# A two-layer attention and convolution trunk on one core: the order inside an attention step, and the parts of the norms' sums

## The chip, the cores and the metric

The kernel runs on one core of one Trainium2 chip. A core has a matrix engine (TensorE, PE in the profile), a vector engine (VectorE, DVE), a scalar engine (ScalarE, ACT), GpSimd (POOL), a queue engine that issues transfers here (SyncE, SP), and 16 DMA engines. The metric is the device time of one execution in microseconds; less is better. Three executions of the kernel before took 1157.65, 1158.02 and 1159.11 us: the median is 1158.02 us.

## The reference

A trunk of two layers works on 256 latent tokens (x, 1024 channels) with 256 context tokens (xc). All values are float32.

```python
for l in range(DEPTH):                                  # DEPTH = 2
    sh1, sc1, g1, sh2, sc2, g2 = split(silu(c) @ w_ada[l] + b_ada[l])      # and the same for the context
    h = rmsnorm(x, norm1_g[l]) * (1 + sc1) + sh1
    p = h @ w_in[l]                                     # conv part, q, k, v, branch gates
    q, k = rope_2d(q), rope_2d(k)                       # 8 heads of 64
    y_conv = silu(layernorm(dwconv31(a * sigmoid(g)))) @ w_conv_out[l]
    y_attn = softmax(q k' / 8 + bias over a window of the latent keys, and all context keys) v @ w_na_out[l]
    x = x + g1 * ((sigmoid(p_gate) * [y_conv, y_attn], summed) @ w_out[l])
    h2 = rmsnorm(x, norm2_g[l]) * (1 + sc2) + sh2
    u = dwconv3(h2 @ w_up[l]);  x = x + g2 * ((silu(u_g) * u_a) @ w_down[l])
    # the context tokens take the same path in layer 0; in layer 1 only their k and v are needed
return rmsnorm(x, final_norm_g)
```

The norms are the sums of squares over all channels of a token: `rsqrt(mean(x*x) + eps)`.

## The kernel before

**Layout.** Channels lie on the 128 partitions (8 tiles for 1024 channels), tokens on the free axis: 512 columns in layer 0 (latents and context are two "streams" of 256 columns) and mostly 256 in layer 1. Each weight comes in units of 1024 columns. SP loads a unit (`raw`, 4 buffers), ScalarE rounds it (`whi`, L148), VectorE takes the remainder (`wlo`, L149), and TensorE multiplies in three matmuls for each tile (`mm3`, L167 to L169: high times high, high times low, low times high; their output tile is called main). The activations are split likewise.

**Order of the work.** The main products are emitted in order, with `slot()` between groups of them. Each call of `slot()` advances every generator in the list `side` by one piece: the attention's steps, the 31 convolution taps, the vector of modulations (adaLN, L194 and L236), and the norms. A scheduler of the tile framework then gives each engine its instruction order; waits between engines follow from the tiles.

**The norm (SumSq L298, rstd L328, norm L362).** Each channel tile's squares (ScalarE, L316) are added to an accumulator (VectorE, L320). The last of the tiles isn't added: it is a second part, squared on VectorE for 256 columns (L312) and on ScalarE for 512. `rstd` sums over the 128 channels by matmuls with a column of ones: for each 128 tokens one product per part, all accumulating (L334; the trace shows each as two instructions). VectorE scales the sum (L336), GpSimd raises it to the power −1/2 (L338), and TensorE spreads it over partitions by transposes (L343). The callers: the first norm (`ss0`), the LayerNorm of the convolution branch (L754, one in each layer), the norms after the output projection (two streams in layer 0, one in layer 1), the ones after the down-projection of layer 0 (two streams), and the final norm, after that of layer 1. A modulated norm (L349) then makes each channel tile's high and low part by L357 to L359.

**Attention (L375).** A pair of heads j gives two or, in layer 0, three items: latent queries 0 to 127, 128 to 255, and all context queries. Scores (L419): six matmuls of 64 rows and 512 columns into two banks of the tag sc (both banks that it has). Softmax (L427 to L435): VectorE adds a bias and takes the maximum, ScalarE does exp and the scaling. Transposes (L469) of the probabilities, with copies by ScalarE (L470). Values (L488): 8 program matmuls of 64 output rows into the tag po (one bank). `step()` (L401) is called once a slot; while items are queued it works only on every second call, and then it does the values due, the transposes due (three calls after the scores), and one queued item's scores, in this order. `ahead` (L391) forces steps until few enough items of the pairs before are left; it is called by `qk` (L657), which makes one pair's q and k on the main products (rotary on VectorE L671 to L674, splits L677 and L678).

**Layer 1's up-projection (L900 on).** Its first four units start on the raw, not yet normalised activations: eight rounds k of 4 products. The generator `sums` (rstd of the norm) is started after round 0 and completed (`whole`) after round 2.

Of the kernel before, what the change touches and what calls it, by code (L numbers as in the profile page):

```python
# [8 lines left out]
F32 = mybir.dt.float32  # L9
# [35 lines left out]
def trunk(ctx: ExitStack, tc: tile.TileContext, xt, cvec, wall, wada, params, bias_t, rope_t, out):  # L45
# [13 lines left out]
    def nm(s):  # L59
        uid[0] += 1  # L60
        return f"{s}_{uid[0]}"
# [3 lines left out]
    def psum(tag="main"):  # L65
        return psp.tile([P, 512], F32, tag=tag, bufs=BANKS[tag], name=nm(tag))
# [7 lines left out]
    def sl(w, i):  # L74
        return w[:, i * P : (i + 1) * P]
# [222 lines left out]
    class SumSq:  # L298


        def __init__(self, T, at):
            self.T, self.n = T, 0
            self.acc = at
            self.parts = [self.acc]

        def add(self, src, last=False):
            T = self.T
            if self.n == 0:
                act.activation(self.acc[:, :T], src, AF.Square)
            elif last and T == S:  # L310
                q = tmp()[:, :T]
                dve.tensor_tensor(q, src, src, ALU.mult)  # L312
                self.parts.append(q)
            else:
                q = tmp()[:, :T]
                act.activation(q, src, AF.Square)  # L316
                if last:
                    self.parts.append(q)
                else:
                    dve.tensor_tensor(self.acc[:, :T], self.acc[:, :T], q, ALU.add)  # L320
            self.n += 1

    def sum_squares(n, T):

        at = tp.tile([P, 512], F32, tag="ss", name=nm("ss"))
        return [SumSq(T, at[:, i * T : (i + 1) * T]) for i in range(n)]

    def rstd(ss, n, bank):  # L328

        nt = ss.T // P  # L330
        pt = psum("pt")
        for t in range(nt):
            for i, p in enumerate(ss.parts):
                pe.matmul(pt[:, t : t + 1], sl(p, t), one, start=i == 0, stop=i == len(ss.parts) - 1)  # L334
        red = small([P, nt], "red")
        mid = dve.tensor_scalar(red, pt[:, :nt], 1.0 / n, EPS, ALU.mult, ALU.add)  # L336
        rs = small([P, nt], "rs")
        pool.tensor_tensor(rs, red, mhalf[:, :nt], ALU.pow)  # L338
        yield mid
        yield  # L340
        pb = psum(bank)
        for t in range(nt):
            pe.transpose(sl(pb, t), rs[:, t : t + 1].to_broadcast([P, P]), ident)  # L343
        return pb
# [30 lines left out]
    class Attention:  # L375
# [4 lines left out]
        def pair(self, j, q, k, bts):  # L380
            po = []
            lat, cx = [None, None], [None, None]
            for qt in range(2):
                self.todo.append((j, qt, q, k, bts[qt], po, lat))
            if self.T > S:
                self.todo.append((j, None, q, k, None, po, cx))

# [3 lines left out]
        def ahead(self, j, n):  # L391

            while sum(it[0] <= j for it in self.todo) > n:
                self.step()

# [4 lines left out]

        def step(self):  # L401
            self.n += 1
            for e in self.soft + self.pv:
                e[0] += 1
            if self.todo and self.n % 2:
                return
            if self.pv and self.pv[0][0] >= 1:
                self.pv.pop(0)[1]()
            if self.soft and self.soft[0][0] >= 3:
                self.turn(*self.soft.pop(0)[1:])  # L410
            if self.todo:
                it = self.todo.pop(0)
                (self.scores if it[1] is not None else self.ctx_scores)(it)

# [5 lines left out]

        def scores(self, it):
            j, qt, q, k, bt, po, pts = it
            out = [psum("sc") for _ in range(2)]
            self.product(out, q, k, slice(qt * P, (qt + 1) * P), slice(0, 2 * S))
            pps = []
# [12 lines left out]

        def ctx_scores(self, it):
            j, qt, q, k, bt, po, pts = it  # L440
            out = [psum("sc") for _ in range(2)]
            for t in range(2):
                self.product([ps[:, t * S : (t + 1) * S] for ps in out], q, k, slice(S + t * P, S + (t + 1) * P), CTX)
            pps = []
# [52 lines left out]

    (ss0,) = sum_squares(1, 2 * S)
    for k in range(KD):
# [4 lines left out]
    for l in range(DEPTH):  # L504
# [5 lines left out]
        with ExitStack() as e1a:  # L510
# [68 lines left out]
            with ExitStack() as e1b:  # L579
# [77 lines left out]
                def qk(j):  # L657

                    att.ahead(j - 2, 0)
                    att.ahead(j - 1, 1 + (T > S))  # L660
                    bts = [eb.tile([P, 2, S], F32, tag="bias", bufs=3, name=nm("bias")) for _ in range(2)]
                    for qt, bt in enumerate(bts):
# [183 lines left out]
        with ExitStack() as e2:  # L846
# [39 lines left out]
            if last:  # L886

                for k in range(KD):
                    for w, ps in zip(first, pss):
                        mm3(ps[:, : S + 2], w[k], h2[0][k][:, RAW], h2[1][k][:, RAW], k == 0, k == KD - 1)  # L890
                    if k == 0:
                        next(sums)
                    if k == 2:
                        pb = whole(sums)
# [37 lines left out]
            if not last:  # L932
                h1 = h_tiles()
            sss = sum_squares(NS, S)
            NB = 0 if last else KD - 2
# [144 lines left out]
```

## Time and profile before

| what | value |
|---|---|
| median of three executions | 1158.02 us |
| the profiled execution | 1160.25 us |
| its span in the profile | 1158.5 us |
| granted TensorE clock, mean | 0.995 |
| read from memory, mean | 161 GB/s |
| share of the transfer queue (q1) of 16 DMA engines' span | 51.3% |

The profiled execution took 1.75 us more than its span, and 2.23 us more than the median. A main matmul starts 0.232 us (512 columns) or 0.118 us (256) after the one before it, though its row shows a longer duration, since matmuls overlap. So what one costs is read from the difference of two starts. The waits of an engine are in its own table: for each wait, the line that waited, the line that released it, the sum, the number and the longest. In a row of the timeline, the first number is the start, the second the duration, x the number of instructions joined to one row, and the brackets hold the idle time before it and what ended it.

### The profile page before, as it was taken

To read this page: it belongs to the slowest core of one execution; us is meant where nothing else is said; L and a number is where in the kernel's file an instruction comes from. 1 tells how busy PE (TensorE), PEld (TensorE's weight loads), DVE (VectorE), ACT (ScalarE), POOL (GpSimd) and SP (SyncE) were. 2 spreads that over 40 slices of the span, in tenths; PEclk is the share of its full clock that TensorE was granted. 3 is DMA by queue.
4 is the path that set the end of the run, shared out by engine and by line. 5 is a ranking of instruction groups with operands and counts; after the bars stand their busy time and mean duration, and the time that the engine had idled before them with its cause. 6 is when DMAs were issued, how large, how long until landed. Compare 5 with 4: busy or idle time off the path is not lost.

```text
span 1158.5 us, 18238 instructions
## 1 busy us (share of the span) xinstructions
PE 1142.6 (99%) x7006; PEld 978.1 (84%) x7006; DVE 951.8 (82%) x1794; ACT 557.6 (48%) x916; POOL 24.6 (2%) x25
## 2 busy tenths in 40 slices
PE   8999999999999999999999999999999999999997
PEld 7677777788769978888888888998879999999996
DVE  3589999968865899988989588789998799888753
ACT  4356667323243354343344222453677567666541
POOL 0000000100000000000000000000000000000000
PEclk8999999999999999999999999999999999999999
DMA  7852313442681345676755455654435474666561
GB/s 242 302 156 79 96 60 110 127 146 60 229 270 60 99 147 171 205 232 201 237 183 160 130 164 180 202 190 132 142 93 163 142 219 125 212 193 183 186 182 55
DMA packets 54230, 187.17 MB, mean 162 GB/s; under 512 B 6272, under 2 KB 6272, under 8 KB 54144
## 3 DMA queue, kind: packets, MB, share of 16 engines
q1 hardware_dynamic: 54144, 186.02, 51.3%
q8 instruction: 55, 0.90, 0.3%
q14 instruction: 31, 0.25, 0.1%
HBM read 184.95 MB, written 1.05 MB: 161 GB/s over the span
## 4 chain that ended last, share of the span: by engine, by line
PE 75%; issue 17%; DVE 3%; DMA 3%; ACT 2%; POOL 0%; SPq 0%; POOLq 0%; DVEq 0%; ACTq 0%
PE main L167 21%; PE main L169 20%; PE main L168 20%; DMA raw<-in_wall 2%; PE po L488 2%; PE sc L419 1%; PE main L589 1%; PE main L590 1%; PE main L591 1%; DVE wlo L149 1%; PE pt L236 1%; PE sc L169 1%; PE pt L334 1%; PE sc L168 1%; PE sc L167 1%
## 5 line engine op out<-in xcount | busy, mean ns | idle before, releaser
L167 PE MATMUL main<-h,whi 128*128 128x256 f32 (+1 forms) x1328 | 450.9, 340 | 1.1 <-ACT whi L148 1.1
L169 PE MATMUL main<-h,wlo 128*128 128x256 f32 (+1 forms) x1328 | 444.1, 335 | 0.1
L168 PE MATMUL main<-h,whi 128*128 128x256 f32 (+1 forms) x1328 | 442.9, 334 | 0.0
L148 ACT CAST whi<-raw 128x1024 fp32r<-128x1024 f32 (+1 forms) x247 | 255.1, 1035 | 341.7 <-PE main L168 171.5
L149 DVE TENSOR_TENSOR wlo<-raw,whi 128x1024 fp32r<-128x1024 f32 (+1 forms) x247 | 296.3, 1204 | 85.8 <-ACT whi L148 84.1
L167 PEld LDWEIGHTS main<-h,whi 128*128 128x128 f32 x1328 | 249.7, 188 | 36.3 <-issue 7.9
L169 PEld LDWEIGHTS main<-h,wlo 128*128 128x128 f32 x1328 | 249.9, 188 | 28.8 <-DVE wlo L149 0.8
L168 PEld LDWEIGHTS main<-h,whi 128*128 128x128 f32 x1328 | 250.2, 188 | 27.0 <-issue 0.6
L259 DVE SCALAR_TENSOR_TENSOR acc<-raw,sil,acc 128x256 f32<-128x256 f32 (+1 forms) x294 | 143.3, 534 | 1.1
L537 DVE SCALAR_TENSOR_TENSOR cb<-u,par,cb 128x512 f32<-128x512 f32 (+1 forms) x240 | 140.2, 611 | 0.6
L167 PE MATMUL main<-fh,whi 128*128 128x256 f32 (+1 forms) x396 | 127.2, 321 | 0.0
L169 PE MATMUL main<-fh,wlo 128*128 128x256 f32 (+1 forms) x396 | 126.4, 319 | 0.0
L168 PE MATMUL main<-fl,whi 128*128 128x256 f32 (+1 forms) x396 | 126.4, 319 | 0.0
L169 PEld LDWEIGHTS main<-fh,wlo 128*128 128x128 f32 x396 | 74.5, 188 | 5.9
L168 PEld LDWEIGHTS main<-fl,whi 128*128 128x128 f32 x396 | 74.5, 188 | 5.7
L167 PEld LDWEIGHTS main<-fh,whi 128*128 128x128 f32 x396 | 74.5, 188 | 5.7
L859 ACT ACTIVATE t<-main,par 128x512 f32<-128x512 f32 (+1 forms) x82 | 50.7, 667 | 13.4 <-PE main L169 13.4
L860 DVE SCALAR_TENSOR_TENSOR t<-main,par,t 128x510 f32<-128x510 f32 (+1 forms) x82 | 47.5, 614 | 1.9 <-ACT t L859 1.5
L863 DVE SCALAR_TENSOR_TENSOR t<-main,par,t 128x510 f32<-128x510 f32 (+1 forms) x82 | 46.8, 610 | 0.0
L799 DVE SCALAR_TENSOR_TENSOR x<-main,mod,x 128x256 f32<-128x256 f32 x48 | 22.2, 480 | 28.1 <-PE main L169 28.1
L358 ACT ACTIVATE h<-t,mod 128x256 fp32r<-128x256 f32 x56 | 25.3, 501 | 35.7 <-DVE t L357 35.7
L878 ACT CAST fh<-t 128x512 fp32r<-128x512 f32 (+1 forms) x44 | 22.5, 513 | 32.6 <-DVE t L875 31.9
(162 smaller groups left out, 1265.0 us busy)
## 6 DMA issues: line engine op xcount, KB each, us to landing
raw<-in_wall SPq DMA_DIRECT2D x239, 512.0 KB, 4.2
raw<-in_wada SPq DMA_DIRECT2D x96, 512.0 KB, 4.3
bias<-in_bias_t SPq DMA_DIRECT2D x16, 256.0 KB, 3.6
x<-in_xt SPq DMA_DIRECT2D x8, 256.0 KB, 4.7
raw<-in_wall SPq DMA_DIRECT2D x8, 256.0 KB, 6.0
out<-t SPq DMA_DIRECT2D x4, 256.0 KB, 2.5
rope<-in_rope_t SPq DMA_DIRECT2D x2, 256.0 KB, 5.3
par<-in_params SPq DMA_DIRECT2D x1, 352.0 KB, 5.6
```

Source lines behind the costliest of these rows:

```text
L148: act.copy(hi[:, c], r[:, c])
L149: dve.tensor_tensor(lo[:, c], r[:, c], hi[:, c].bitcast(F32), ALU.subtract)
L167: pe.matmul(ps, w[0], xh, start=start, stop=False)
L168: pe.matmul(ps, w[0], xl, start=False, stop=False)
L169: pe.matmul(ps, w[1], xh, start=False, stop=stop)
L259: dve.scalar_tensor_tensor(a, w, c, a, ALU.mult, ALU.add)
L358: act.activation(hi[:, c], y[:, c], AF.Identity, bias=b)
L488: pe.matmul(po[i * HD : (i + 1) * HD, c], self.V[kt][:, h * HD : (h + 1) * HD], pts[i][:, kt - kts[0], :], start=kt == kts[0], stop=kt == ...
L537: dve.scalar_tensor_tensor(cb[j], src, w, cb[j], ALU.mult, ALU.add)
L859: act.activation(c, pv_, AF.Identity, bias=pr(l, FDB + t, 1), scale=w[1])
L860: dve.scalar_tensor_tensor(c[:, :, 1:], pv_[:, :, : S - 1], w[0], c[:, :, 1:], ALU.mult, ALU.add)
L863: dve.scalar_tensor_tensor(c[:, :, : S - 1], pv_[:, :, 1:], w[2], c[:, :, : S - 1], ALU.mult, ALU.add)
```

## The change

It has three parts.

1. A sum of squares has a second part only for the first norm and the final one (`apart`). For the seven others, the last tile's squares are taken on ScalarE and added to the accumulator on VectorE like those of the other tiles, and `rstd` has one part. The loops of `rstd` change places.
2. `Attention.step` issues the scores' products first, then the values, then the transposes; the softmax of the scores comes last. An item's scores come at the earliest two calls of `step` after it was queued, unless `ahead` forces them (`now`). In `qk`, the threshold of the pair before is 2 in both layers (1 in layer 1 until now), and layer 1 has four buffers for the bias in place of three.
3. In layer 1's up-projection, `sums` is started after round 1 and completed after round 3.

```diff
@@ -298,8 +298,8 @@
     class SumSq:
 
 
-        def __init__(self, T, at):
-            self.T, self.n = T, 0
+        def __init__(self, T, at, apart):
+            self.T, self.n, self.apart = T, 0, apart
             self.acc = at
             self.parts = [self.acc]
 
@@ -307,31 +307,34 @@
             T = self.T
             if self.n == 0:
                 act.activation(self.acc[:, :T], src, AF.Square)
-            elif last and T == S:
+            elif last and T == S and self.apart:
                 q = tmp()[:, :T]
                 dve.tensor_tensor(q, src, src, ALU.mult)
                 self.parts.append(q)
             else:
                 q = tmp()[:, :T]
                 act.activation(q, src, AF.Square)
-                if last:
+                if last and self.apart:
                     self.parts.append(q)
                 else:
                     dve.tensor_tensor(self.acc[:, :T], self.acc[:, :T], q, ALU.add)
             self.n += 1
 
-    def sum_squares(n, T):
+    def sum_squares(n, T, apart=False):
 
         at = tp.tile([P, 512], F32, tag="ss", name=nm("ss"))
-        return [SumSq(T, at[:, i * T : (i + 1) * T]) for i in range(n)]
+        return [SumSq(T, at[:, i * T : (i + 1) * T], apart) for i in range(n)]
 
     def rstd(ss, n, bank):
 
         nt = ss.T // P
         pt = psum("pt")
-        for t in range(nt):
-            for i, p in enumerate(ss.parts):
-                pe.matmul(pt[:, t : t + 1], sl(p, t), one, start=i == 0, stop=i == len(ss.parts) - 1)
+        for i, p in enumerate(ss.parts):
+            for t in range(nt):
+                pe.matmul(
+                    pt[:, t : t + 1], sl(p, t), one, start=i == 0 and t == 0, stop=i == len(ss.parts) - 1,
+                    skip_group_check=True,
+                )
         red = small([P, nt], "red")
         mid = dve.tensor_scalar(red, pt[:, :nt], 1.0 / n, EPS, ALU.mult, ALU.add)
         rs = small([P, nt], "rs")
@@ -381,9 +384,9 @@
             po = []
             lat, cx = [None, None], [None, None]
             for qt in range(2):
-                self.todo.append((j, qt, q, k, bts[qt], po, lat))
+                self.todo.append((j, qt, q, k, bts[qt], po, lat, self.n))
             if self.T > S:
-                self.todo.append((j, None, q, k, None, po, cx))
+                self.todo.append((j, None, q, k, None, po, cx, self.n))
 
         def busy(self):
             return self.todo or self.soft or self.pv
@@ -391,26 +394,31 @@
         def ahead(self, j, n):
 
             while sum(it[0] <= j for it in self.todo) > n:
-                self.step()
+                self.step(True)
 
         def run(self):
             while True:
                 self.step()
                 yield
 
-        def step(self):
+        def step(self, now=False):
+
+
             self.n += 1
             for e in self.soft + self.pv:
                 e[0] += 1
-            if self.todo and self.n % 2:
+            if self.todo and self.n % 2 and not now:
                 return
+            it = None
+            if self.todo and (now or self.n - self.todo[0][-1] >= 2):
+                *it, _ = self.todo.pop(0)
+                out = self.products(it)
             if self.pv and self.pv[0][0] >= 1:
                 self.pv.pop(0)[1]()
             if self.soft and self.soft[0][0] >= 3:
                 self.turn(*self.soft.pop(0)[1:])
-            if self.todo:
-                it = self.todo.pop(0)
-                (self.scores if it[1] is not None else self.ctx_scores)(it)
+            if it:
+                (self.scores if it[1] is not None else self.ctx_scores)(it, out)
 
         def product(self, out, q, k, c, d):
 
@@ -418,10 +426,18 @@
                 for o, r in zip(out, HALF):
                     pe.matmul(o, q[r, a, c], k[r, b, d], start=n == 0, stop=n == 2)
 
-        def scores(self, it):
+        def products(self, it):
             j, qt, q, k, bt, po, pts = it
             out = [psum("sc") for _ in range(2)]
-            self.product(out, q, k, slice(qt * P, (qt + 1) * P), slice(0, 2 * S))
+            if qt is not None:
+                self.product(out, q, k, slice(qt * P, (qt + 1) * P), slice(0, 2 * S))
+            else:
+                for t in range(2):
+                    self.product([ps[:, t * S : (t + 1) * S] for ps in out], q, k, slice(S + t * P, S + (t + 1) * P), CTX)
+            return out
+
+        def scores(self, it, out):
+            j, qt, q, k, bt, po, pts = it
             pps = []
             for i, ps in enumerate(out):
                 dve.tensor_tensor(ps[:, :S], ps[:, :S], bt[:, i, :], ALU.add)
@@ -436,11 +452,7 @@
                 pps.append(pp)
             self.soft.append([0, it, pps])
 
-        def ctx_scores(self, it):
-            j, qt, q, k, bt, po, pts = it
-            out = [psum("sc") for _ in range(2)]
-            for t in range(2):
-                self.product([ps[:, t * S : (t + 1) * S] for ps in out], q, k, slice(S + t * P, S + (t + 1) * P), CTX)
+        def ctx_scores(self, it, out):
             pps = []
             for ps in out:
                 mx = small([P, 2], "mx2")
@@ -495,7 +507,7 @@
                 dve.tensor_tensor(self.ol[j][:, c], po[:, c], self.oh[j][:, c].bitcast(F32), ALU.subtract)
 
 
-    (ss0,) = sum_squares(1, 2 * S)
+    (ss0,) = sum_squares(1, 2 * S, True)
     for k in range(KD):
         sp.dma_start(x[k], xt[k])
         ss0.add(x[k], k == KD - 1)
@@ -657,8 +669,8 @@
                 def qk(j):
 
                     att.ahead(j - 2, 0)
-                    att.ahead(j - 1, 1 + (T > S))
-                    bts = [eb.tile([P, 2, S], F32, tag="bias", bufs=3, name=nm("bias")) for _ in range(2)]
+                    att.ahead(j - 1, 2)
+                    bts = [eb.tile([P, 2, S], F32, tag="bias", bufs=4 if last else 3, name=nm("bias")) for _ in range(2)]
                     for qt, bt in enumerate(bts):
                         with tc.issue_after(lastdma[0].ins):
                             sp.dma_start(bt, bias_t[l, j, :, qt])
@@ -888,9 +900,9 @@
                 for k in range(KD):
                     for w, ps in zip(first, pss):
                         mm3(ps[:, : S + 2], w[k], h2[0][k][:, RAW], h2[1][k][:, RAW], k == 0, k == KD - 1)
-                    if k == 0:
+                    if k == 1:
                         next(sums)
-                    if k == 2:
+                    if k == 3:
                         pb = whole(sums)
                 for k in range(KD):
                     modulated(l, pb, 4, 3, k, h2, (0,))
@@ -931,7 +943,7 @@
 
             if not last:
                 h1 = h_tiles()
-            sss = sum_squares(NS, S)
+            sss = sum_squares(NS, S, last)
             NB = 0 if last else KD - 2
             if not last:
                 ad = ada_vector([(1, j, True, 2) for j in range(0, 8)])
```

On the engines' instruction orders, the change has these effects beside the removed L334. In layer 0 the attention's steps stay in their places, with the order inside each changed. In layer 1 the scores and values stand in 10 separate stretches of TensorE's order where there were 13. One adaLN product (L194) in layer 0, after the attention, stands in two halves. In the norm after layer 1's output projection, 24 main matmuls stand between round 1's end and the sum, and 24 more between it and L343. In layer 1's feed-forward, some weight casts (L148, L149) stand behind the convolution and gate operations of the same step that they stood ahead of.

## The prediction

> **What bounds the kernel now.** I read the busy times first, then the chain that ended last, the waits of TensorE (engine, its line, what released it; us in total, times, longest), and the groups by line.
>
> ```profile
> span 1158.5 us, 18238 instructions
> PE 1142.6 (99%) x7006; PEld 978.1 (84%) x7006; DVE 951.8 (82%) x1794; ACT 557.6 (48%) x916; POOL 24.6 (2%) x25
> ...
> PE 75%; issue 17%; DVE 3%; DMA 3%; ACT 2%; POOL 0%; SPq 0%; POOLq 0%; DVEq 0%; ACTq 0%
> ```
>
> ```profile
> PE po L343 <- POOL rs L338: 1.9, 2, 1.1
> ```
>
> TensorE is the bound: 99% busy, 75% of the chain plus 17% in which it only issues. So only two things can shorten the span: fewer or better packed TensorE instructions, or the few waits in its table. The waits within the change's reach are these 1.9 us (L343 for the norm's power on POOL) and 1.6 us of L334 for the squares of L312 (the third row of the next fence); the 1.3 us that L334 waits for L320 is the start-up norm, which keeps its parts. DVE is second with 82%, and an edit that makes it late shows as new waits.
>
> **Part 1: one part instead of two.** Seven norms lose the second part: the LayerNorm of each layer, the norm after the output projection of layer 0 (both streams) and of layer 1, and the one after layer 0's down-projection (both streams). The rows of their matmuls (L334) and of what makes their input, busy us and mean ns:
>
> ```profile
> L320 DVE TENSOR_TENSOR ss<-ss,t 128x256 f32<-128x256 f32 (+1 forms) x46 | 20.9, 468 | 11.7 <-ACT t L316 11.2
> ...
> L316 ACT ACTIVATE t<-x 128x256 f32<-128x256 f32 (+1 forms) x43 | 18.7, 448 | 30.6 <-DVE x L799 28.7 <-DMA x<-in_xt 1.6
> ...
> L334 PE MATMUL pt<-one,t 128*128 128x1 f32 x44 | 8.1, 254 | 1.6 <-DVE t L312 1.6
> ...
> L334 PE MATMUL pt<-one,ss 128*128 128x1 f32 x44 | 7.5, 239 | 1.3 <-DVE ss L320 1.3
> ```
>
> The 239 to 254 ns are latency, and instructions overlap. The price on TensorE is the pitch, from the timeline of layer 0's LayerNorm (first of its 16 instructions, then the next main matmul):
>
> ```profile
> 269.06 0.28 PE L334 MATMUL pt<-one,ss 128*128 128x1 f32 x2
> ...
> 270.76 0.48 PE L167 MATMUL main<-h,whi 128*128 128x512 f32 x1
> ```
>
> (270.76 − 269.06)/16 = 0.106 us, and the entry into the next matmul stays. Removed are 8 instructions here (4 columns of 128 tokens, two instructions for each product in the trace) and 4 at each of six other sites, 32 in all, at 0.106 to 0.112: at most **3.5 us**. From this comes what the longer input chain gives back: a square on VectorE (L312, 0.42 us in the rows below) becomes a square on ScalarE (0.45) and then an add on VectorE (0.47), so the input is later by about 0.5 us plus what is queued on either engine. Where it arrives behind TensorE, the removed 0.45 us turns into a wait. Site by site, with the instruction order of both kernels beside the trace:
>
> - LayerNorm of layer 0, 8 removed: its input is some 0.3 us ahead of 269.06, so −0.9. LayerNorm of layer 1, 4 removed, input 3 us ahead (it joins two long casts, but in front of them): −0.45.
> - After the output projection of layer 0: the first stream's chain starts with this update of x, with ScalarE idle and VectorE's queue empty; 365.65 + 0.48 + 0.45 + 0.47 and small hand-overs give 367.1, against an arrival of TensorE at 367.0, so −0.25 of 0.45.
>
> ```profile
> 365.65 0.48 DVE L799 SCALAR_TENSOR_TENSOR x<-main,mod,x 128x256 f32<-128x256 f32 x1 [1.39 <-PE main L169]
> ```
>
> - There, the second stream's add falls behind a long cast (L149, 1.2 us), and its matmuls now stand 11 main matmuls later: about even, −0.45.
> - After layer 0's down-projection, first stream. Rows of VectorE, POOL and TensorE:
>
> ```profile
> 744.77 1.23 DVE L149 TENSOR_TENSOR wlo<-raw,whi 128x1024 fp32r<-128x1024 f32 x1
> ```
>
> ```profile
> 746.29 1.68 POOL L338 TENSOR_TENSOR rs<-red,mhalf 128x2 f32<-128x2 f32 x1 [361.35 <-DVE red L336]
> ```
>
> ```profile
> 744.99 0.28 PE L334 MATMUL pt<-one,ss 128*128 128x1 f32 x2
> ...
> 748.74 0.38 PE L343 MATMUL po<-ident,rs 128*128 128x128 f32 x2
> ```
>
> The add stands behind the cast that ends at 746.00, so it is ready at 746.4; TensorE arrives ten matmuls later than now, at 746.2. Then the reduction waits for one more cast (to 747.6), the power follows, and the broadcast L343 comes at 748.6 to 748.7, as now: −0.1.
>
> - The same, second stream:
>
> ```profile
> 763.29 0.38 PE L334 MATMUL pt<-one,t 128*128 128x1 f32 x2
> ...
> 766.54 0.43 PE L343 MATMUL po<-ident,rs 128*128 128x128 f32 x2 [0.78 <-POOL rs L338]
> ```
>
> ```profile
> 762.82 0.42 DVE L312 TENSOR_TENSOR t<-x 128x256 f32<-128x256 f32 x1
> 764.58 0.16 DVE L336 TENSOR_SCALAR red<-pt 128x2 f32<-128x2 f32 x1 [1.34 <-PE sc L169]
> 764.71 1.23 DVE L149 TENSOR_TENSOR wlo<-raw,whi 128x1024 fp32r<-128x1024 f32 x1
> ```
>
> L312 stands behind a cast already, and ScalarE squares meanwhile, so the add ends when L312 did (763.24). Four instructions follow at 763.29 in place of six, so the reduction is 0.22 earlier, and with it the power, if that is still slow beside the cast: L343 at 766.3, −0.25. If the power got ahead of the cast it would take the 0.70 us that it takes beside an idle VectorE:
>
> ```profile
> 368.11 0.70 POOL L338 TENSOR_TENSOR rs<-red,mhalf 128x2 f32<-128x2 f32 x1 [95.74 <-DVE red L336]
> ```
>
> Then L343 would wait for nothing, and this site would give −0.9. I take −0.25, since ScalarE's cast moves forward with TensorE and the long L149 with it. [...]
>
> - After the output projection of layer 1:
>
> ```profile
> 959.93 0.38 PE L334 MATMUL pt<-one,ss 128*128 128x1 f32 x2
> ...
> 962.19 0.38 PE L334 MATMUL pt<-one,t 128*128 128x1 f32 x2 [0.69 <-DVE t L312]
> ```
>
> ```profile
> 961.71 0.42 DVE L312 TENSOR_TENSOR t<-x 128x256 f32<-128x256 f32 x1
> ...
> 963.13 2.35 DVE L149 TENSOR_TENSOR wlo<-raw,whi 128x1024 fp32r<-128x1024 f32 x2
> ```
>
> The square waits for a cast on ScalarE, so the add ends near 962.3 and the stall grows from 0.7 to about 1.1 us, with three more matmuls done ahead of it. The reduction then stands behind a cast and the power beside the next: L343 some 1.1 us later, but with 48 matmuls done since in place of 36 (12 × 0.118 = 1.4): −0.3.
>
> Sum of part 1: −0.9 − 0.45 − 0.25 − 0.45 − 0.1 − 0.25 − 0.3 = **−2.7**.
>
> **Part 2: the order in attention.** In layer 0 the same steps are left; only their order within a step changes, and the number of times that TensorE leaves its 128-row main matmuls stays: 0. In layer 1 the stretches of scores or values fall from 13 to 10. What a lone one costs, and the one that now waits for its operand in the middle:
>
> ```profile
> 818.61 0.28 PE L168 MATMUL main<-h,whi 128*128 128x256 f32 x1
> 818.72 0.28 PE L169 MATMUL main<-h,wlo 128*128 128x256 f32 x1
> 818.93 0.96 PE L419 MATMUL sc<-qk,qk 64*128 64x512 f32 x6
> 819.82 0.38 PE L167 MATMUL main<-h,whi 128*128 128x256 f32 x1
> 820.04 0.28 PE L168 MATMUL main<-h,whi 128*128 128x256 f32 x1
> ```
>
> ```profile
> 833.75 0.28 PE L169 MATMUL main<-h,wlo 128*128 128x256 f32 x1
> 834.20 0.50 PE L419 MATMUL sc<-qk,qk 64*128 64x512 f32 x2 [0.17 <-ACT qk L677]
> ...
> 834.95 0.73 PE L419 MATMUL sc<-qk,qk 64*128 64x512 f32 x4
> 835.61 0.39 PE L168 MATMUL main<-h,whi 128*128 128x256 f32 x1
> ```
>
> A lone stretch takes 819.82 − 818.72 = 1.10; the broken one 835.61 − 833.75 = 1.86, of which one main matmul is 0.12 (818.72 − 818.61, 0.118 over longer runs). With the pair's scores two slots later the operand is there: −0.64. Two other scores now stand beside values and no longer alone, which saves the entry (0.21 − 0.12) and the slow first matmul (0.22 − 0.12) each: −0.4. The later scores delay VectorE's softmax by up to 3 us and the attention's last output (L495) by 6; first and last start of its two instructions and of the first product that reads it:
>
> ```profile
> L168 PEld LDWEIGHTS main<-ol,whi x32: 187/188/192, 912.5 to 923.8; 128*128 128x128 f32 x32
> ...
> L495 DVE TENSOR_TENSOR ol<-po,oh x2: 418/422/425, 883.8 to 894.6; 128x256 fp32r<-128x256 f32 x2
> ```
>
> From 894.6 to 912.5 are 18 us, which hide it. If VectorE's queue passed it on to the weight casts, the cover would be gone (rival below). Sum of part 2: **−1.0**. The two bias loads that start earlier lie in a fourth buffer and cost nothing.
>
> **Part 3: smaller moves.** In the stage after layer 0's attention, one product of the adaLN vector (L194) falls into two halves with main matmuls between. From the chain, a whole one and a half:
>
> ```profile
> 308.87 1.00 PE sc L194 x16
> 313.02 0.61 PE sc L194 x8
> ```
>
> Two halves cost 2 × 0.61 against 1.00: +0.2. The later start of the last layer's sums is in part 1. In the last layer's feed-forward the weight casts stand some conversions later in the queues; each waits for its buffer now, four units of 24 matmuls ahead of use, which hides it.
>
> **Sum:** −2.7 − 1.0 + 0.2 = −3.5 us. The profiled execution took 1160.25 us (1.75 outside its span), 2.2 above the median of the runs; it would take 1156.75, and the median 1158.02 − 3.5 = **1154.5**.
>
> **Rivals.** About 0.2% (2.3 us) is what a measurement of this kernel can tell from no change.
>
> *The removed matmuls come back as waits* (no change). Squares that now pass ScalarE, VectorE and two hand-overs come late at all six short sites, and four instructions of 0.11 only become idle time. For it: L312's waits of 1.6 us exist already. Against it: both LayerNorms have slack. Part 1 shrinks to −1.35, part 2 to what the broken stretch gives, −0.6, with +0.2: 1156.3; if the power too meets a cast at two sites (+0.5 each) 1157.2.
>
> *VectorE gets the bound in layer 1's attention* (slower). From 777 to 888 us it is busy 109.6 of 111:
>
> ```profile
> 777.00:888.00 111.00, 110.83 (x737) 94.55 (x736) 109.64 (x254) 66.41 (x125) 3.23 (x2) 1.00 0.43 129
> ```
>
> (TensorE, its loads, VectorE are the first three busy times.) Scores issued first hold their two banks while values and transposes follow, and the transposes need the softmax three slots later. If VectorE's delay of up to 3.3 us exceeds the spare of a step (about 6.5 us between steps, some 5 of softmax), every one of the eight steps waits 0.4 to 1 us: +3 to +8, less part 1: +0.5 to +5, about 1161. It decides when a step's delay passes some 1.5 us. Against it: no wait of a transpose shows now, and the casts stand earlier in VectorE's queue, not later.
>
> *All falls well:* the power gets ahead of the casts, and every site gives its 0.45: −3.5 − 0.9 − 1.0 + 0.2 = −5.2, 1152.8.
>
> **How the numbers follow.** Forecast (1153.5 to 1155.6) 0.45, all well 0.15, back as waits 0.25, slower 0.15. The all-well case and nearly all of the forecast lie beyond −2.3 us, so faster 0.6. Of the slower case a small part lies within 2.3 us: same 0.26, slower 0.14. The range of 1152.5 to 1158.8 takes in all but most of the slower case and the far edge of the best.
>
> **What would show it.** L334 with 12 instructions on second parts and 44 on sums (44 and 44 now); L312's wait gone, a wait of L334 on L320 in its place of at most 1.5 us in sum beside the 1.3; L343's wait under 1.5; the scores of layer 1 without a wait or a matmul inside, near 841; no new wait of L469 or L488. Waits of the transposes on softmax, or of main matmuls on L149 between 820 and 900, would make the forecast wrong.

## The result and the profile after

The changed kernel took 1152.06 us (median of 6 executions, 1150.76 to 1154.11), the kernel before 1158.57 in the same measurement: a ratio of 0.9946, 95% interval 0.9932 to 0.9960. A second measurement of the same two kernels, on another occasion, gave 1153.88 to 1158.86 and 0.9958 (0.9945 to 0.9971). By the medians the change is faster by 6.5 us in the first measurement and by 5.0 in the second, where 3.5 were forecast. The second (e8) had been expected at 0.9954 from the first trace.

The page of the changed kernel (1152.23 us, span 1150.4), the same lines as before, and below them the clock row of each kernel's page:

```profile
span 1150.4 us, 18199 instructions
PE 1134.2 (99%) x6974; PEld 970.1 (84%) x6974; DVE 952.7 (83%) x1795; ACT 560.9 (49%) x923; POOL 20.0 (2%) x25
...
PEclk9999999999999999999999999999999999999999
...
PE 76%; issue 17%; DMA 3%; DVE 2%; ACT 1%; POOL 0%; SPq 0%; POOLq 0%; DVEq 0%; ACTq 0%
```

```profile
PEclk8999999999999999999999999999999999999999
```

TensorE has 32 instructions fewer and is still the bound. Its waits in the changed kernel:

```profile
PE pt L334 <- DVE ss L320: 2.3, 3, 1.3
PE sc L123 <- POOL ident masks.py:199: 1.8, 1, 1.8
PE po L346 <- POOL rs L341: 1.6, 2, 1.1
...
PE pt L334 <- DVE t L312: 0.7, 1, 0.7
```

Beside the 1.3 us of the start, the sums wait for adds for 1.0 us in two places, and the one wait for L312 left is the final norm's. The groups by line confirm the counts, 44 and 12:

```profile
L320 DVE TENSOR_TENSOR ss<-ss,t 128x256 f32<-128x256 f32 (+1 forms) x53 | 24.2, 467 | 11.1 <-ACT t L316 10.5
...
L334 PE MATMUL pt<-one,ss 128*128 128x1 f32 x44 | 5.9, 243 | 2.4 <-DVE ss L320 2.3
...
L334 PE MATMUL pt<-one,t 128*128 128x1 f32 x12 | 1.6, 252 | 0.7 <-DVE t L312 0.7
```

The two spans differ by 8.1 us, 1.6 more than the medians. All traces here have the same 5988 main matmuls, and in the same order, but for 59 of them behind layer 0's attention (between places 938 and 997), which stand otherwise in the eight traces with the new sums. So a stretch of the kernel can be timed from the start of one of them to the start of another, and compared between traces. This gives the following table (us; "start" is up to main matmul 180, "LN" the LayerNorms, "out" and "down" the norms after the output and down-projections):

| run | start | attention, layer 0 | LN 0 | out 0, both | down, 1st | down, 2nd | attention, layer 1 | LN 1 | out 1 |
|---|---|---|---|---|---|---|---|---|---|
| before | 74.43 | 148.25 | 16.61 | 30.84 | 15.36 | 29.00 | 89.96 | 15.31 | 16.98 |
| before, longer warm-up (e4) | 72.24 | 148.28 | 16.61 | 30.84 | 15.36 | 29.12 | 89.95 | 15.31 | 16.49 |
| changed | 71.61 | 147.63 | 15.71 | 30.20 | 15.29 | 28.73 | 88.70 | 14.87 | 16.02 |
| changed again (e8) | 73.25 | 147.63 | 15.71 | 30.18 | 15.28 | 28.79 | 88.71 | 14.87 | 15.72 |
| changed, longer warm-up (e3) | 71.96 | 147.63 | 15.71 | 30.18 | 15.28 | 28.77 | 88.71 | 14.87 | 15.47 |
| sums only (e1) | 72.51 | 148.26 | 15.71 | 30.19 | 15.28 | 28.74 | 89.74 | 14.87 | 15.78 |
| attention only (e2) | 73.51 | 147.63 | 16.61 | 30.84 | 15.36 | 27.88 | 88.70 | 15.31 | 16.57 |
| order only (e6) | 72.31 | 147.63 | 16.61 | 30.84 | 15.36 | 28.17 | 89.86 | 15.31 | 16.13 |
| delay only (e7) | 74.29 | 148.28 | 16.61 | 30.84 | 15.36 | 29.05 | 89.28 | 15.31 | 16.69 |
| changed, no delay (e13) | 71.66 | 147.63 | 15.72 | 30.18 | 15.28 | 28.66 | 89.59 | 14.87 | 15.74 |
| changed, sums start as before (e5) | 74.11 | 147.63 | 15.71 | 30.21 | 15.28 | 28.68 | 88.71 | 14.87 | 16.33 |
| changed, 2nd part kept at out 1 (e9) | 75.58 | 147.63 | 15.71 | 30.19 | 15.28 | 28.63 | 88.71 | 14.87 | 15.47 |
| changed, 2nd part kept at down (e12) | 71.16 | 147.63 | 15.71 | 30.21 | 15.36 | 27.95 | 88.70 | 14.87 | 15.72 |

From main matmul 180 to the start of the last one, the two traces of the kernel before take 1074.08 and 1073.82 us, the three of the changed kernel 1069.12, 1069.20 and 1068.44: **−5.0 us**. (e3 and e4 differ from the two kernels only in their warm-up.) Of the table's columns, only the start and "out 1" vary from one execution of the same kernel to another by more than 0.15.

Behind the last main matmul comes the final norm, which no column holds. It keeps both its parts, but the exchanged loops of `rstd` move two instructions on the accumulator (`ss`) ahead of the wait for the square (`t`). Kernel before, the sum and its reduction:

```profile
1148.63 0.28 PE L334 MATMUL pt<-one,ss 128*128 128x1 f32 x2
1149.83 0.38 PE L334 MATMUL pt<-one,t 128*128 128x1 f32 x2 [0.92 <-DVE t L312]
1150.08 0.36 PE L334 MATMUL pt<-one,ss 128*128 128x1 f32 x2
1150.30 0.36 PE L334 MATMUL pt<-one,t 128*128 128x1 f32 x2
```

```profile
1150.77 0.16 DVE L336 TENSOR_SCALAR red<-pt 128x2 f32<-128x2 f32 x1 [0.99 <-PE pt L334]
```

The changed kernel:

```profile
1140.85 0.50 PE L334 MATMUL pt<-one,ss 128*128 128x1 f32 x4
1142.04 0.61 PE L334 MATMUL pt<-one,t 128*128 128x1 f32 x4 [0.70 <-DVE t L312]
```

```profile
1142.76 0.16 DVE L339 TENSOR_SCALAR red<-pt 128x2 f32<-128x2 f32 x1 [0.77 <-PE pt L334]
```

From the first instruction on the square to the reduction it is 0.94 us before and 0.72 after, so **0.2 us** more are gained there.

The start differs by 2.8 us between the two profiles, and most of that goes with the clock. Granted clock is the third value from the right; kernel before:

```profile
12.00:13.00 1.00, 1.00 (x11) 1.00 (x11) 0.00 (x0) 0.00 (x0) 0.00 (x0) 1.00 1.06 408
13.00:14.00 1.00, 1.00 (x10) 0.98 (x10) 0.00 (x0) 0.00 (x0) 0.00 (x0) 0.68 1.06 420
...
19.00:20.00 1.00, 1.00 (x6) 1.00 (x6) 0.82 (x3) 0.67 (x2) 0.00 (x0) 0.50 0.30 119
20.00:21.00 1.00, 1.00 (x7) 0.87 (x6) 1.00 (x3) 0.71 (x2) 0.00 (x0) 0.91 0.02 8
```

The changed kernel in the same stretch:

```profile
12.00:13.00 1.00, 1.00 (x11) 0.98 (x10) 0.00 (x0) 0.00 (x0) 0.00 (x0) 1.00 1.06 393
13.00:14.00 1.00, 1.00 (x18) 0.42 (x17) 0.16 (x1) 0.51 (x1) 0.65 (x1) 1.00 1.03 410
```

A mean of 0.68 and of 0.91 places the changes inside their microseconds: half speed lasts from about 13.4 to 20.2 us in one and is absent from the other. In the four traces without such a drop the start takes 71.2 to 72.0 us, in the four with 3.4 us of half speed 72.2 to 73.5, and in the five with 6.8 us 73.3 to 75.6. The changed kernel has the drop too: "changed again" is at half speed for 6.8 us. But all four traces without it have the new order of the first norm's products (four of eight), and none of the five with the old order. The mean granted clock shows no such difference: 0.9952 over 51 executions with the new order and the same warm-up, 0.9954 over 68 of the kernel before. So whether the change makes the drop rarer stays open; the means speak against it.

### The profile page after: what moved, and what is told of

Read it like the earlier page. It is cut to its first block, busy times and chain, and to the rows that moved or that the text cites. A ratio compares the mean times of both kernels' runs of the same rounds, so it can differ in the third digit from the quotient of the medians.

```text
span 1150.4 us, 18199 instructions
## 1 busy us (share of the span) xinstructions
PE 1134.2 (99%) x6974; PEld 970.1 (84%) x6974; DVE 952.7 (83%) x1795; ACT 560.9 (49%) x923; POOL 20.0 (2%) x25
## 4 chain that ended last, share of the span: by engine, by line
PE 76%; issue 17%; DMA 3%; DVE 2%; ACT 1%; POOL 0%; SPq 0%; POOLq 0%; DVEq 0%; ACTq 0%
PE main L167 21%; PE main L169 21%; PE main L168 21%; DMA raw<-in_wall 2%; PE po L500 2%; PE sc L427 2%; PE main L601 1%; PE main L603 1%; PE main L602 1%; PE pt L236 1%; DVE wlo L149 1%; ACT whi L148 1%; PE pt L481 1%; PE sc L169 1%; PE sc L167 1%
## 5 line engine op out<-in xcount | busy, mean ns | idle before, releaser
L148 ACT CAST whi<-raw 128x1024 fp32r<-128x1024 f32 (+1 forms) x247 | 255.0, 1035 | 337.0 <-PE main L168 171.6
L149 DVE TENSOR_TENSOR wlo<-raw,whi 128x1024 fp32r<-128x1024 f32 (+1 forms) x247 | 296.9, 1204 | 82.5 <-ACT whi L148 81.1
L871 ACT ACTIVATE t<-main,par 128x512 f32<-128x512 f32 (+1 forms) x82 | 50.7, 667 | 13.5 <-PE main L169 13.4
```

What stands on the lines that cost most here:

```text
L148: act.copy(hi[:, c], r[:, c])
L149: dve.tensor_tensor(lo[:, c], r[:, c], hi[:, c].bitcast(F32), ALU.subtract)
L871: act.activation(c, pv_, AF.Identity, bias=pr(l, FDB + t, 1), scale=w[1])
```

## The experiments

My theory after the result (A): the gain is what the table shows stretch by stretch, and what the medians add to it is the start's chance. Rivals stand with each run.

**e1, the sums alone** (the attention's class and `qk` as before; two places of the edit, against the changed kernel):

```diff
-        def step(self, now=False):
+        def step(self):
 ...
-                    att.ahead(j - 1, 2)
+                    att.ahead(j - 1, 1 + (T > S))
```

> The kernel before with the one-part sums and the later start of the last layer's sums, attention untouched. Theory A (the gain is what the trace shows behind the first 20 us, site by site, and the start's difference is the chance of the clock): the norms' sites give 0.89 + 0.64 + 0.07 + 0.27 + 0.45 + 0.95 = 3.3 us, less 0.2 for the adaLN product in two halves: 3.1 us faster than before, 0.27% (1155.4 beside 1158.5). Rival B (the change also makes the clock's drop at the start rarer, by the other order of the first norm's products): 1.5 us more, so 4.6 us faster.

Ratio 0.9973 (0.9963 to 0.9984), 3.1 us. The stretches of the sums give −0.90 − 0.65 − 0.08 − 0.32 − 0.44 and at "out 1" about −0.8, 3.2 us, and layer 1's attention, whose code is as before, another 0.2: theory A. The mean granted clock of its ten executions was 0.995, like that of the kernel before, and its trace has the drop for 3.4 us, so nothing in this run speaks for rival B.

**e2, the attention alone** (the reverse of e1's edit, on the kernel before; in part):

```diff
+        def step(self, now=False):
 ...
+            if self.todo and (now or self.n - self.todo[0][-1] >= 2):
+                *it, _ = self.todo.pop(0)
+                out = self.products(it)
```

> The kernel before with the new attention step alone. Theory A: 1.26 us in layer 1 and some 0.25 us in layer 0, together 1.5 us faster (1157.0 beside 1158.5). Rival B says the same here, since the first norm is as before: 1.5 us. If the attention's part is larger than the trace showed, 2.5 us or more.

Ratio 0.9976 (0.9966 to 0.9986), 2.8 us. Attention itself gives −0.63 and −1.25. But "down, 2nd" is 1.1 shorter too, where no sum was changed: this I hadn't expected, and e6 and e12 follow it. Mostly because of it, the two halves of the change are not additive: from main matmul 180 to the last, e1 is 3.5 us shorter than the kernel before, e2 3.1, and the changed kernel 5.0.

**e3 and e4, a longer warm-up** (both kernels):

```diff
-    busy(28)
+    busy(33)
```

> The changed kernel with 33 in place of 28 warming matmuls at the start (they compute nothing that is used), so that TensorE is idle for some 0.4 us and not 1.4 before the first norm's sums. All other instructions keep their order. If the clock's drop at the start depends on that idle stretch, the spread between executions shrinks and the median falls by 0 to 1.5 us: 1150.6 to 1152.1. If it does not, 1152.1 and the same spread of 3 us.

> The kernel before with the same 33 warming matmuls. Theory A: the distance to the run with the longer warm-up of the changed kernel is the 4.7 to 5.0 us of the trace behind the first 20 us; rival B: the same distance here, but 6.3 us without the warm-up. The median of this run is 1155.5 to 1158.5.

e3: 1152.46 us, 0.9948 (0.9932 to 0.9963) of the kernel before; e4: 1157.30, 0.9993 (0.9984 to 1.0003). The distance is 4.8 us, as theory A says, and the two traces differ by 5.4 from main matmul 180 to the last. The mean granted clock of the executions rose from 0.9954 to 0.9972 in the kernel before. That mean also holds the half-speed stretch that every trace here shows at its end (6.8 to 10.0 us), so it doesn't tell how often the start drops, and e4's trace still drops for 3.4 us. In time the gain is within the interval, and the spread stayed.

**e5, the sums started as before** and **e9, the second part kept at that one norm** (changed kernel):

```diff
-                    if k == 1:
+                    if k == 0:
                         next(sums)
-                    if k == 3:
+                    if k == 2:
```

> The changed kernel, with the last layer's sums started after round 0 and completed after round 2 as before. Theory A (the input of the sum after layer 1's output projection comes at a fixed time, set by VectorE's queue, and the 12 matmuls moved ahead of it fill the wait): TensorE waits 12 x 0.118 = 1.4 us longer for the add, some 2.1 us in all, and the run is 1.4 us slower than the changed kernel, 1153.6 beside 1152.2. Rival: the one-part sum alone made the gain there, and this run equals the changed kernel within 0.3 us.

```diff
-                sss = sum_squares(NS, S)
+                sss = sum_squares(NS, S, last)
```

> The changed kernel with the second part kept at one site, the norm after the output projection of layer 1 (its start stays after round 1). Theory A (the add of the last tile comes no later than its square did, since both stand behind the same long cast on VectorE; what goes is four instructions): this site loses 4 x 0.11 = 0.45 us and TensorE waits as long as in the changed kernel, 0.7 us: the run is 0.4 to 0.6 us slower than the changed kernel in the trace. Rival (the later start of the sums made the gain of 1 us there): no difference, within 0.2 us.

e5: ratio 0.9967 (0.9956 to 0.9978). "Out 1" takes 16.33, against 15.47 to 16.02 in the six traces with the change's sums and start there, and 16.13 to 16.98 in the five with the old ones; the loss is 0.6 and not 1.4, for the scheduler put the sum 3 main matmuls earlier, not 12 (21 stand ahead of it and 15 between it and L346, in place of 24 and 24). e9: ratio 0.9952 (0.9932 to 0.9971), "out 1" 15.47, no slower than with one part. So theory A fails here and its rival holds: most of this site's 0.8 us, some 0.6, comes from the later start of the sums. What the removed instructions give (0.24 between e5 and the mean before, nothing in e9) is less than the site's spread, with one trace for each run. The sum in the changed kernel, in e5 and in e9 (start, duration, and the wait in brackets):

```profile
955.13 0.60 PE L334 MATMUL pt<-one,ss 128*128 128x1 f32 x4 [0.66 <-DVE ss L320]
```

```profile
958.15 0.61 PE L334 MATMUL pt<-one,ss 128*128 128x1 f32 x4 [0.75 <-DVE ss L320]
```

```profile
958.23 0.50 PE L334 MATMUL pt<-one,ss 128*128 128x1 f32 x4
958.59 0.58 PE L334 MATMUL pt<-one,t 128*128 128x1 f32 x4
```

With one part TensorE waits for an add; with two and the late start it does four more instructions instead of waiting.

**e6, the order alone** (scores first, nothing delayed), and **e7, the delay alone** (scores last, in their old place), on the kernel before (of both edits the lines that matter):

```diff
+            it = None
+            if self.todo:
+                *it, _ = self.todo.pop(0)
+                out = self.products(it)
             if self.pv and self.pv[0][0] >= 1:
 ...
```

> The kernel before with the new order inside a step alone (scores, values, transposes), without the two slots of delay, thresholds and bias buffers as before. Theory A: it takes all of layer 0's gain, 0.6 us (the values that stood out of step at 167 us, 0.35, and 0.05 at each of five steps), and none of layer 1's, since the broken scores stay and the stretches are 13: 0.6 us faster than before. Rival: the order also lets softmax start earlier where VectorE is the bound, and layer 1 gains 1 us with it.

```diff
-            if self.todo:
+            if self.todo and (now or self.n - self.todo[0][-1] >= 2):
```

> The kernel before with the two slots of delay alone (with the forced steps, the threshold 2 and four bias buffers), the order inside a step as before (values, transposes, scores). Theory A: layer 0 as before, the values out of step stay; layer 1 loses the broken stretch and two lone ones: 0.9 to 1.2 us faster than before. The run with all of the attention's change is then this and the order alone, 1.9 us in sum. Rival: without the new order the delayed scores come behind values and transposes and the softmax is late, which gives a wait of the transposes, 0 or slower.

e6: 0.9988 (0.9978 to 0.9998); layer 0's attention takes 147.63, all of the 0.63; layer 1's only 0.1 less. Theory A for attention; "down, 2nd" is 0.9 shorter besides and "out 1" 0.4, and the trace gains 1.8 in all. e7: 0.9997 (0.9987 to 1.0007), no difference in the median, but its trace has layer 1's attention at 89.28, 0.67 less where 0.9 to 1.2 were expected, and no other column moves beyond its spread; that is under what the medians can tell. Together order and delay give 1.25 (e2), so 0.5 come only with both. **e13, the changed kernel without the delay,** shows the other side (thresholds and bias buffers go back too):

```diff
-            if self.todo and (now or self.n - self.todo[0][-1] >= 2):
+            if self.todo:
                 *it, _ = self.todo.pop(0)
```

> The changed kernel without the two slots of delay (thresholds and bias buffers as before), the order of scores, values, transposes kept. Theory A: layer 0 keeps its gain, layer 1 loses the 1.24 us of attention: between 0.7 (what the delay alone gave) and 1.24 us slower than the changed kernel in the trace. Rival: the delay gives nothing by itself, as its median beside the kernel before said (1159.1 to 1158.9): within 0.3 us.

0.9953 (0.9935 to 0.9970), layer 1's attention 89.59, 0.89 more than with the delay: theory A.

**e12, the second part kept after the down-projection of layer 0** (changed kernel):

```diff
-            sss = sum_squares(NS, S, last)
+            sss = sum_squares(NS, S, True)
```

> The changed kernel with the second part kept at the two norms after the down-projection of layer 0, as in the kernel before. In the runs with the new order of attention and these norms as before, the power on GpSimd started ahead of the long cast on VectorE and took 0.70 us; with one part it started 0.03 us behind it and took 1.75. Theory A (who starts first decides): the power is again ahead of the cast, the broadcast comes without a wait, and the run is 0.3 to 0.7 us faster than the changed kernel in the trace, in spite of eight more instructions. Rival (four instructions for each site are what counts): 0.3 to 0.4 us slower, as the first stream lost 0.1 and the second 0.3.

"Down, 2nd" takes 27.95 in place of 28.73: theory A, with eight more instructions on TensorE. VectorE and the power on GpSimd in the changed kernel:

```profile
759.36 0.16 DVE L339 TENSOR_SCALAR red<-pt 128x2 f32<-128x2 f32 x1 [0.83 <-PE pt L334]
759.57 1.22 DVE L149 TENSOR_TENSOR wlo<-raw,whi 128x1024 fp32r<-128x1024 f32 x1
```

```profile
759.60 1.75 POOL L341 TENSOR_TENSOR rs<-red,mhalf 128x2 f32<-128x2 f32 x1 [2.67 <-DVE red L339]
```

The same in e12:

```profile
759.13 0.16 DVE L339 TENSOR_SCALAR red<-pt 128x2 f32<-128x2 f32 x1 [0.77 <-PE pt L334]
759.75 1.23 DVE L149 TENSOR_TENSOR wlo<-raw,whi 128x1024 fp32r<-128x1024 f32 x1 [0.47 <-ACT whi L148]
```

```profile
759.37 0.70 POOL L341 TENSOR_TENSOR rs<-red,mhalf 128x2 f32<-128x2 f32 x1 [2.62 <-DVE red L339]
```

The cast starts 0.03 us ahead of the power in one, 0.38 behind it in the other, and the power takes 1.75 or 0.70. In e6 it was the same as in e12:

```profile
762.14 0.16 DVE L336 TENSOR_SCALAR red<-pt 128x2 f32<-128x2 f32 x1 [0.99 <-PE pt L334]
762.63 1.23 DVE L149 TENSOR_TENSOR wlo<-raw,whi 128x1024 fp32r<-128x1024 f32 x1 [0.33 <-ACT whi L148]
```

```profile
762.38 0.70 POOL L338 TENSOR_TENSOR rs<-red,mhalf 128x2 f32<-128x2 f32 x1 [2.85 <-DVE red L336]
```

The reduction is released by the sum there, and in the kernel before by the main matmul behind it (the row at 764.58 in the prediction), which puts the power behind the cast. Why the release differs is not settled. By the starts that the traces give, who starts first doesn't settle the power's time alone either. In e1, after layer 1's output projection, the power starts 0.01 us ahead of the cast and is slow all the same:

```profile
958.97 1.78 POOL L341 TENSOR_TENSOR rs<-red,mhalf 128x2 f32<-128x2 f32 x1 [52.58 <-DVE red L339]
958.98 1.23 DVE L149 TENSOR_TENSOR wlo<-raw,whi 128x1024 fp32r<-128x1024 f32 x1
```

The fast ones beside a cast lead it by 0.25 us (e6), 0.31 (e2) and 0.38 (e12). From main matmul 180 to the last, e12's trace takes 1068.26 us, the changed kernel's 1068.44 to 1069.20. Its ratio, 0.9949 (0.9932 to 0.9967), can't tell that from the changed kernel's.

## Why the prediction was wrong

The direction held, and so did most steps. The sum was too small: −3.5 for a measured −5.0 in the traces up to the last main matmul, and −6.5 and −5.0 in the medians; 1152.06 lies 0.4 below the range. The steps that failed are four: the stall at "out 1", forecast to grow (−0.3 for the site, −0.8 measured); the 0 for layer 0's attention (−0.63); the final norm, which the sum doesn't hold (−0.2); and the size of layer 1's attention (−1.0, −1.25 measured). The rival "all falls well" has nearly the measured gain, −5.2, but this is no proof of it: its mechanism, the power ahead of the cast at the down-projection's second stream and 0.45 at every other site, did not occur: the down-projection's two streams gave 0.08 and 0.30. Step by step:

- *The price of L334 and both LayerNorms: right.* LayerNorm of layer 0, forecast −0.9, measured −0.90; of layer 1, −0.45 and −0.44. The changed kernel's row beside the next main matmul gives (266.42 − 265.61)/8 = 0.10 us for each instruction:

```profile
265.61 0.95 PE L334 MATMUL pt<-one,ss 128*128 128x1 f32 x8
266.42 0.48 PE L167 MATMUL main<-h,whi 128*128 128x512 f32 x1
```

- *Layer 0's output and down-projections: right.* −0.25 − 0.45 = −0.70 forecast, −0.65 measured; −0.1 and −0.08; −0.25 and −0.30. In the last, the power did stay behind the cast, though only by 0.03 us. The stronger outcome, which the prediction priced at −0.9, occurred where the attention's order is new and the sum keeps two parts (e2, e6, e12: −0.9 to −1.2).
- *"The add ends near 962.3 and the stall grows from 0.7 to about 1.1 us": wrong.* This step gave −0.3 for "out 1"; the six traces with the change's sums and start there (changed, e8, e3, e1, e13, e12) have a mean of 15.74, the five without either 16.57, so **−0.8**. The square of the last tile waits for ScalarE's cast, as I said, but the add can't start before VectorE's long cast either, which the old square also waited for. So the add ends when the square did. The rows of VectorE in the changed kernel, cast and add:

```profile
953.53 1.22 DVE L149 TENSOR_TENSOR wlo<-raw,whi 128x1024 fp32r<-128x1024 f32 x1
954.66 0.42 DVE L320 TENSOR_TENSOR ss<-ss,t 128x256 f32<-128x256 f32 x1
```

  And the cast ahead of the square at 961.71 in the kernel before:

```profile
960.58 1.22 DVE L149 TENSOR_TENSOR wlo<-raw,whi 128x1024 fp32r<-128x1024 f32 x1
```

  The square stood 1.13 us behind the start of its cast, and the add stands 1.13 us behind it here. The stall stayed at 0.2 to 0.7, and the matmuls moved ahead of it by the later start, which the prediction counted as filler for a longer wait, became gain. e5 (16.33, above all six) and e9 (15.47) point to this start as the cause of most of it.
- *"In layer 0 ... 0": wrong.* It measured −0.63 and depends on the order alone (e6). I counted how often TensorE leaves the main matmuls and didn't look at the operands of those stretches. In the kernel before, one set of values starts at 167.38 while ScalarE still copies the second head's probabilities:

```profile
167.09 0.58 ACT L470 COPY pT<-main 128x512 f32<-128x512 f32 x1
```

```profile
167.38 2.29 PE L488 MATMUL po<-pT,V 128*64 128x256 f32 x16
```

  In the changed kernel the copy that belongs to these values is done 1.8 us before they start:

```profile
161.94 0.60 ACT L482 COPY pT<-main 128x512 f32<-128x512 f32 x1
```

```profile
164.35 1.95 PE L500 MATMUL po<-pT,V 128*64 128x256 f32 x16
```

  The copy ends 0.29 us after the values' start and costs 0.34; the wait table doesn't list it. The other 0.3 us are 0.04 at each of seven steps.
- *The final norm: left out.* The prediction gave the exchange of `rstd`'s loops no term, since this norm keeps its parts. It also counted all 1.6 us of L334's wait for L312 as within reach and their end as a sign, though 0.9 of them are this norm's: 0.7 are left.
- *Layer 1's attention: right in its mechanism, short in its size.* −1.0 forecast, −1.25 measured. The stretch from main matmul 3480 through the broken scores gave 0.71 (forecast 0.64), and the two scores that now stand beside values 0.28 and 0.26 (forecast 0.19 each). The broken scores are whole, the transposes directly behind them; 830.06 is some 836 in the time of the profile before, where I had said near 841:

```profile
829.85 0.28 PE L169 MATMUL main<-h,wlo 128*128 128x256 f32 x1
830.06 0.96 PE L427 MATMUL sc<-qk,qk 64*128 64x512 f32 x6
830.95 0.66 PE L481 MATMUL pt<-ident,pp 128*128 128x128 f32 x4
```

  No wait of transposes or values on softmax appeared, so the slower rival was wrong: VectorE's later softmax was covered. The wait of L343 (now L346) on the power, 1.6 us, did not fall under 1.5 as I had said; 1.1 of it are the final norm's.
- *The adaLN product in two halves, +0.2: in line, but not shown.* The stretch from main matmul 900 to 1200 takes 77.05 us in the mean of the five traces with the old sums (76.72 to 77.46) and 77.27 in that of the eight with the new ones (76.98 to 77.97), so the spread is larger than the difference.
- *The profiled execution.* Its start held the half-speed clock, and its "out 1" was the slowest of all. Both vary among executions; the forecast rested on differences and wasn't hurt. Whether the first measurement's 6.5 us contain more than the 5.0, the final norm's 0.2 and chance at the start is not settled; the second gave 5.0.

## What to carry to other kernels

A removed instruction on the bound engine was worth its pitch only where its input came early (0.11 us each at the LayerNorms, 0.02 at the down-projection's first stream); where the input was the limit, moving the consumer later in the order gained more than making it cheaper (at "out 1": two parts and the later start, 15.47 us in e9; one part and the early start, 16.33 in e5; one trace each). When an operation takes another's place, ask which queue both stood behind, and not only how long the new chain is. And time the same instruction in two traces: it shows 0.1 us where medians of ten executions show 1.

## What the runs showed of the hardware that I had not expected

- The granted clock drops at the start in nine of the 13 traces: in the kernel before to half speed (0.50) for 6.8 us, though TensorE's idle time there was only 1.26 us, followed by 1.5 us of one-column matmuls. The idle time alone doesn't decide it: e1 drops after 0.20 us, e13 doesn't after 1.52, and the changed kernel's trace doesn't after 1.29 us and 1.9 us of one-column matmuls. What decides it, no run here shows.
- The power on GpSimd took 1.75 us when it started 0.03 us behind the cast (changed kernel), and 0.69 to 0.70 when it led by 0.25 to 0.38 (e6, e2, e12). The power that led by 0.01 us took 1.78 (e1). No run here shows why it is slow there.
- The values of two heads run as pairs: in the kernel before, from 136.02, the two matmuls of a pair start 0.007 us apart, and after the first a pair every 0.216 us. In the stretch that began with one operand late (167.38), starts are 0.088 and 0.128 us apart in turn, and 16 instructions took 2.21 us up to the next main matmul, against 1.87 in the changed kernel: they did not fall back into step.
